# A four-layer trunk on one core: the first layer's sums of x two jobs later, two u tiles moved up, and the means of the two long pooling spans six places later

## The chip, the core and the metric

The kernel runs on one core of a Trainium2 chip. The core's engines each work through a queue of their own: TensorE (PE; its weight loads are shown as PEld), VectorE (DVE), ScalarE (ACT), GpSimd (POOL) and SyncE (SP), which here only issues DMAs. An instruction that waits for a semaphore holds up everything behind it in its engine's queue. The metric is the device time of one execution in microseconds (us).

## The reference

The reference is a trunk of four residual layers over 512 tokens of width 1024: pooling, gated convolution, latent attention, pooling; a last RMSNorm closes it. What matters here is the pooling layer (layers 1 and 4):

```python
xn = rms_norm(x, pool_norm[j])
u, z = jnp.split(xn @ w_in, 2, axis=-1)          # 1024 -> 2048 + 2048
for g, w in enumerate((2, 4, 8, 16)):            # four groups of 512 channels
    mean = trailing_mean(u[:, :, g], w)
    pooled.append(mean - u[:, :, g])
mixed = einsum('bsgc,gcd->bsgd', pooled, w_grp) * scale
x = x + (mixed * silu(z)) @ w_out
```

All inputs and the output are fp32.

## The kernel before

Activations lie with channels on the 128 partitions and the 512 tokens along the free dimension. Each fp32 operand of a matmul is split into a high part `h` (ACT copies it to fp32r) and a low part `l` (DVE subtracts), and each product is made of three matmuls (`mm3`, L260). So every weight chunk goes through ACT's `high` (L248) and DVE's `low` (L251) before PE can use it.

**Jobs and positions.** A `Stream` is a list of jobs. One job is a chunk of weights with its matmuls, and it has eight positions (0 to 7), one ahead of each k step. `step` (L215) loads the weights of the jobs one and two ahead, puts the preparation of the next job's weights into the positions of this job (high at 1, low at 2), and runs the matmuls. Everything that is to be done beside the matmuls is put down in a dictionary from position to functions; position 8 + p is position p of the next job, and so on. Work that is put down at the end of a job counts from the start of the next one. At one position the preparation of weights comes first. Within `Stream.run` the order in which PE, DVE and ACT get their instructions is the order in which this code issues them (`manual_schedule`, L231); the orders of POOL and SP are made by the scheduler.

**Chunk jobs** (`tile`, 24 matmuls with 512 columns) make one tile of u: 128 channels by 512 tokens. **Pair jobs** (`pair`, `seven`, L432) make two tiles of z at once out of seven products instead of eight, 84 matmuls with 256 columns. For those, x is needed in summed forms, `XNorm.forms` (L354): for each of four pairs of x tiles ACT makes g (L362), DVE four sums d1 and d2 (L366 to L369), ACT their high parts fh (L375) and DVE their low parts fl (L385). The weights need sums too, `prepare_pair` (L389): one block is loaded twice (s13, L117), a second one is added to it by an accumulating DMA that POOL issues (L121), and DVE and ACT make ah/al, sh/sl, ch/cl (positions 4 to 7) and, out of two further sums, th/tl (positions 10 and 11). The seven products use them in the order A11 (ah, al), S1 (sh, sl), A22, A12 (ch, cl), S2 and S4 (th, tl), S3.

**A pooling layer** (`pool_layer`, L590) runs jobs in the order of `ORDER`: uGI is tile I of group G of u, zGI a pair of z tiles, mGI half of the group's mixing matmul, h0 and h1 the two halves of the output projection (eight jobs each). In the first layer u00 and u01 are made together as the first job (`first_two`), and z00 and z01 are two chunk jobs each, since the summed forms aren't there yet. z10 is the first job that needs them.

**After a u tile** (`post_u`, L606): DVE multiplies it by the norm (`mul`, L583), POOL makes the trailing sums with one to four adds (`add`, L620; one for group 0, four for group 3), DVE makes the mean and subtracts the token (`mean`, L626 to L628), ACT makes the high part plh (L631) and DVE the low part pll (L634). The mixing matmul of the group reads plh and pll.

All these intermediate tiles, x with its split parts and the summed forms among them, come out of one set of 70 buffers (`up`, L69). Raw weight chunks have four buffers (`wr`).

The first two layers' jobs are in stream s1. The last layer's are in s2, whose jobs up to m21 are issued outside `manual_schedule` (L1262), so that there the scheduler makes DVE's, ACT's and PE's order too; from z30 on the order is the written one.

Of the kernel before, what the change touches and what calls it, by code (L numbers as in the profile page):

```python
# [64 lines left out]
def trunk_kernel(ctx: ExitStack, tc: tile.TileContext, a):  # L65
# [9 lines left out]
    def nm(s):  # L75
        cnt[0] += 1
        return f"{s}_{cnt[0]}"

    def ut(s, dt=F32, w=S):
        return up.tile([P, S + PAD], dt, tag="u", name=nm(s))[:, :w]  # L80
# [10 lines left out]
    def ps(s):  # L91
        return pp.tile([P, S], F32, tag="ps", name=nm(s))

    def f(t):
        return t.bitcast(F32)
# [55 lines left out]
    def pcol(name, i, p=None):  # L151
        return (par if p is None else p)[:, PC[name][0] + i : PC[name][0] + i + 1]
# [107 lines left out]
    def mm3(out, ah, al, bh, bl, first, last):  # L260
        nc.tensor.matmul(out, ah, bh, start=first, stop=False)  # L261
        nc.tensor.matmul(out, ah, bl, start=False, stop=False)  # L262
        nc.tensor.matmul(out, al, bh, start=False, stop=last)  # L263
# [318 lines left out]
    def tmul(dst, src, R):  # L582
        nc.vector.tensor_tensor(out=dst, in0=src, in1=R, op=ALU.mult)  # L583


    LATE = "u20 u21 m10 u22 u23 m11 h0 z20 z21 u30 u31 m20 u32 u33 m21 z30 z31 m30 m31 h1"
    ORDER = ("u00 u01 u02 u03 u10 u11 u12 u13 z00 z01 m00 m01 z10 z11 " + LATE,
             "u00 u01 u02 u03 z00 z01 u10 u11 m00 u12 u13 m01 z10 z11 " + LATE)

    def pool_layer(stream, j, xn, half, mid=None, at=(1, 3), pre=None):  # L590
# [12 lines left out]
        for g, w in enumerate(WINDOWS):  # L603
            pooled, szs = [], []

            def post_u(t, sign, g=g, w=w, pooled=pooled):  # L606
                u = up.tile([P, S + PAD], F32, tag="u", name=nm("u"))
                h, l = ut("plh", F32R), ut("pll", F32R)
                pooled.append((h, l))
                sums = []  # L610

                def mul():
                    nc.gpsimd.memset(u[:, :PAD], 0.0)
                    tmul(u[:, PAD:], t, ly.R[sign])
                    sums.append(u)

                def add(d):
                    cur, nx = sums[0], up.tile([P, S + PAD], F32, tag="u", name=nm("s"))
                    lo = 2 * d - 1
                    nc.gpsimd.tensor_tensor(out=nx[:, lo:], in0=cur[:, lo:], in1=cur[:, lo - d : S + PAD - d], op=ALU.add)  # L620
                    sums[0] = nx

                def mean():
                    cur, pd = sums[0], sums[0][:, PAD:]
                    hd = sp.tile([P, PAD], F32, tag="hd", name=nm("hd"))
                    nc.vector.tensor_tensor(out=hd, in0=cur[:, PAD : 2 * PAD], in1=con[:, C_INV + PAD * g : C_INV + PAD * (g + 1)], op=ALU.mult)  # L626
                    nc.vector.scalar_tensor_tensor(out=pd, in0=cur[:, PAD:], scalar=1.0 / w, in1=u[:, PAD:], op0=ALU.mult, op1=ALU.subtract)
                    nc.vector.tensor_tensor(out=pd[:, :PAD], in0=hd, in1=u[:, PAD : 2 * PAD], op=ALU.subtract)  # L628

                def high():  # L630
                    nc.scalar.activation(h, sums[0][:, PAD:], AF.Copy)  # L631

                def low():
                    nc.vector.tensor_tensor(out=l, in0=sums[0][:, PAD:], in1=f(h), op=ALU.subtract)  # L634

                adds = [lambda q=q: add(2**q) for q in range(g + 1)]
                return {0: [mul, *adds], 12: [mean], 14: [high], 16: [low]}

            def post_z(t, sign, szs=szs, plain=g == 0 and pre is not None):
                sz = ut("sz") if plain else t  # L640

                def scale():
                    tmul(sz, t, ly.R[sign])

                def gate():
                    nc.scalar.activation(sz, sz, AF.Silu)
                    szs.append(sz)

                return {0: [scale], 3: [gate]}

            def mix(mm, g=g, pooled=pooled, szs=szs):
                def run(wl, now):
                    for e in range(2):
                        i = 2 * mm + e
                        pm = ps("pm")
                        for k in range(4):
                            now(4 * e + k)
                            c = slice(k * 2 * P + e * P, k * 2 * P + (e + 1) * P)
                            mm3(pm, wl[0][:, c], wl[1][:, c], *pooled[k], first=k == 0, last=k == 3)
                        y, h, l = szs[i], ut("yh", F32R), ut("yl", F32R)  # L660
                        ys[g // 2].append((h, l))

                        def gated(pm=pm, y=y, i=i):
                            nc.vector.scalar_tensor_tensor(out=y, in0=pm, scalar=pcol(f"pool_scale{j}", 4 * g + i), in1=y, op0=ALU.mult, op1=ALU.mult)

                        def high(h=h, y=y):
                            nc.scalar.activation(h, y, AF.Copy)  # L667

                        def low(h=h, l=l, y=y):
                            nc.vector.tensor_tensor(out=l, in0=y, in1=f(h), op=ALU.subtract)  # L670

                        (stream.later if e else now).put({0: [gated], 3: [high], 4: [low]} if e else {5: [gated], 6: [high], 7: [low]})

                stream.add(CHUNK, wg[g, mm], run)

            for i in range(4):
                u_[g, i] = lambda g=g, i=i, post_u=post_u: ly.tile(stream, wu[4 * g + i], post_u)
            for i in range(2):
                z_[g, i] = lambda g=g, i=i, post_z=post_z: (ly.pair if g or pre is None else two_tiles)(stream, wz[2 * g + i], (post_z, post_z), mid and mid(g, i))
                m_[g, i] = lambda mix=mix, i=i: mix(i)  # L680
            if g == 0 and pre is not None:
                u_[0, 0] = lambda post_u=post_u: stream.add(None, None, lambda w, now: ly.done(stream, *[(post_u, t, 1) for t in pre()]))
                u_[0, 1] = lambda: None
        for c in ORDER[j].split():
            if c[0] == "h":
# [420 lines left out]
    s1, s2 = Stream(), Stream()  # L1106
# [7 lines left out]
    xn0 = XNorm("pool_norm0")  # L1114
# [3 lines left out]
    def split_w(m, hf, c, copy):  # L1118
        src, (h, l) = raw0[m, hf][:, c], w0[m, hf]
        copy(h[:, c], src)  # L1120
        nc.vector.tensor_tensor(out=l[:, c], in0=src, in1=f(h)[:, c], op=ALU.subtract)

    def first_two():

        pre = [ps("pt") for _ in range(2)]
        for k in range(KD):
            hf = k // 4
            c = slice((k % 4) * P, (k % 4 + 1) * P)
            for m in range(2):
                if k % 4 == 0:  # L1130
                    w0[m, hf] = ut("wh", F32R), ut("wl", F32R)
            if k == 0:
                split_w(0, 0, slice(0, P), nc.vector.tensor_copy)
                xn0.plain(k)
                split_w(1, 0, slice(0, P), nc.vector.tensor_copy)
                for m in range(2):
                    split_w(m, 0, slice(P, S), nc.vector.tensor_copy if m == 0 else nc.scalar.copy)
            else:
                xn0.plain(k)
                if k == 4:  # L1140
                    for m in range(2):
                        split_w(m, 1, slice(0, S), nc.scalar.copy)
            for m in range(2):
                wh, wl = w0[m, hf]
                if k == m == 0:
                    xh, xl = xn0.xs[0]
                    nc.tensor.matmul(pre[0], wh[:, c], xh, start=True, stop=False)
                    nc.tensor.matmul(pre[0], wl[:, c], xh, start=False, stop=False)
                    nc.tensor.matmul(pre[0], wh[:, c], xl, start=False, stop=False)
                    continue  # L1150
                mm3(pre[m], wh[:, c], wl[:, c], *xn0.xs[k], first=(k == 0), last=(k == KD - 1))
            if k >= 2:
                xn0.st.add(xt[k - 2])

        for m in range(KD - 2, KD):
            s1.later.put({0: [lambda m=m: xn0.st.add(xt[m])]})
        s1.later.put({3: [xn0.st.close]})
        for kk in range(KK):
            s1.later.put(xn0.forms(kk), 48 + 8 * kk)
        return pre  # L1160

    pool_layer(s1, 0, xn0, half, at=(3, 5), pre=first_two)
# [221 lines left out]
```

## Time and profile before

| what | value |
|---|---|
| time, median of 3 runs | 1491.59 us |
| the three runs | 1488.02, 1491.59, 1491.71 us |
| the profiled execution | 1488.14 us |
| its span, first to last instruction | 1486.4 us |
| mean granted clock of TensorE | 0.992 |

The profile was taken from one execution, which was near the faster of the runs. Its span leaves out 1.7 us around it. A row of the timeline reads: start, duration, engine, line, operation, output<-inputs, shapes, count, and in brackets how long the engine was idle before and what ended that. A row of the table of stretches reads: the stretch, its length, the busy time of PE (and number of instructions), PEld, DVE, ACT and POOL, then TensorE's granted clock, the DMA share and GB/s. A row of the view of waits reads: engine, what it was to do, for whom it waited: total, times, longest.

PE starts the first layer's jobs at these times (us from the start of the span): z00's two tiles at 54.93 and 60.46, z01's at 72.16 and 80.28, m00 at 87.08, z10 at 98.21, z11 at 108.13, u20 at 118.08, h0 at 151.41, m21 at 247.30, z30 at 252.82, m30 at 278.49.

### The profile page before, as it was taken

To read this page: it belongs to the slowest core of one execution; us is meant where nothing else is said; L and a number is where in the kernel's file an instruction comes from. 1 tells how busy PE (TensorE), PEld (TensorE's weight loads), DVE (VectorE), ACT (ScalarE), POOL (GpSimd) and SP (SyncE) were. 2 spreads that over 40 slices of the span, in tenths; PEclk is the share of its full clock that TensorE was granted. 3 is DMA by queue.
4 is the path that set the end of the run, shared out by engine and by line. 5 is a ranking of instruction groups with operands and counts; after the bars stand their busy time and mean duration, and the time that the engine had idled before them with its cause. 6 is when DMAs were issued, how large, how long until landed. Compare 5 with 4: busy or idle time off the path is not lost. (4 is left out here: it accounts for less than half of the span.)

```text
span 1486.4 us, 22441 instructions
## 1 busy us (share of the span) xinstructions
PE 1442.5 (97%) x8560; PEld 1271.0 (86%) x8560; DVE 1090.3 (73%) x1771; ACT 685.1 (46%) x1174; POOL 254.7 (17%) x291
## 2 busy tenths in 40 slices
PE   9899998999999999999999999999999999999898
PEld 6688797987999889999879987888888898888786
DVE  6885556749999879999688977677755588655773
ACT  4353242435555426555355655555633355323352
POOL 3402206021001000010211001111201132310502
PEclk9999999999999999999999999999999999999999
DMA  6143344425777357776236742122122443343431
GB/s 231 57 121 121 101 127 99 142 75 123 178 185 192 129 135 184 187 183 177 93 97 170 169 137 82 44 69 85 44 85 85 114 128 97 131 114 107 119 114 57
DMA packets 65147, 181.71 MB, mean 122 GB/s; under 512 B 8080, under 2 KB 8080, under 8 KB 65040
## 3 DMA queue, kind: packets, MB, share of 16 engines
q1 hardware_dynamic: 56688, 151.44, 33.4%
q0 software_dynamic: 7488, 27.27, 10.7%
q10 hardware_dynamic: 864, 1.57, 0.3%
q8 instruction: 67, 1.10, 0.3%
q14 instruction: 40, 0.33, 0.1%
HBM read 173.70 MB, written 2.10 MB: 118 GB/s over the span
## 5 line engine op out<-in xcount | busy, mean ns | idle before, releaser
L251 DVE TENSOR_TENSOR wl<-wr,wh 128x1024 fp32r<-128x1024 f32 (+1 forms) x140 | 173.3, 1238 | 52.5 <-ACT wh L248 52.0
L248 ACT ACTIVATE wh<-wr 128x1024 fp32r<-128x1024 f32 (+1 forms) x140 | 144.4, 1034 | 139.6 <-PE o L262 47.7
L263 PE MATMUL o<-yh,wl 128*128 128x512 f32 x384 | 151.1, 394 | 1.9 <-DVE wl L251 1.9
L262 PE MATMUL o<-yl,wh 128*128 128x512 f32 x384 | 151.2, 394 | 0.2 <-DVE yl L670 0.2
L261 PE MATMUL pt<-xh,wh 128*128 128x512 f32 x367 | 145.9, 398 | 5.6 <-ACT wh L248 5.2
L261 PE MATMUL o<-yh,wh 128*128 128x512 f32 x384 | 151.2, 394 | 0.1
L263 PE MATMUL pt<-xh,wl 128*128 128x512 f32 x367 | 145.1, 396 | 4.0 <-DVE wl L251 3.9
L262 PE MATMUL pt<-xl,wh 128*128 128x512 f32 x367 | 145.4, 396 | 1.0 <-DVE xl L352 0.9
L443 ACT ACTIVATE kept<-bv 128x256 f32<-128x256 f32 x52 | 19.9, 382 | 169.5 <-PE bv L429 137.4
L263 PEld LDWEIGHTS o<-yh,wl 128*128 128x128 f32 x384 | 72.1, 188 | 19.4 <-DVE wl L251 2.8
L261 PEld LDWEIGHTS pt<-xh,wh 128*128 128x128 f32 x367 | 69.4, 189 | 22.3 <-ACT wh L248 6.1
L263 PEld LDWEIGHTS pt<-xh,wl 128*128 128x128 f32 x367 | 69.3, 189 | 22.4 <-DVE wl L251 6.9
L262 PEld LDWEIGHTS o<-yl,wh 128*128 128x128 f32 x384 | 72.2, 188 | 17.1 <-DVE yl L670 0.5
L261 PEld LDWEIGHTS o<-yh,wh 128*128 128x128 f32 x384 | 72.0, 188 | 16.9 <-ACT yh L667 0.5
L262 PEld LDWEIGHTS pt<-xl,wh 128*128 128x128 f32 x367 | 69.5, 189 | 17.8 <-DVE xl L352 2.6
L399 DVE TENSOR_TENSOR sl<-s,sh 128x1024 fp32r<-128x1024 f32 x52 | 64.6, 1242 | 22.1 <-ACT sh L396 22.1
L121 POOL DMA_DIRECT2D s<-in_conv_in x30 | 26.0, 866 | 310.0 <-DMA s<-in_conv_in 95.4
L285 POOL TENSOR_TENSOR sq<-sq,sq 128x512 f32<-128x512 f32 x25 | 41.2, 1649 | 203.4 <-ACT sq L279 203.1
L399 DVE TENSOR_TENSOR al<-wr,ah 128x1024 fp32r<-128x1024 f32 x52 | 64.2, 1234 | 15.4 <-ACT ah L396 13.4
L620 POOL TENSOR_TENSOR s<-u 128x527 f32<-128x527 f32 x32 | 48.9, 1527 | 154.3 <-DVE u L583 146.1
L620 POOL TENSOR_TENSOR s<-s 128x525 f32<-128x525 f32 (+2 forms) x48 | 66.1, 1377 | 14.5 <-PE pm L262 11.2
L443 ACT ACTIVATE kept<-bx 128x512 f32<-128x512 f32 x104 | 50.9, 490 | 37.1 <-PE bx L429 37.1
(308 smaller groups left out, 4576.2 us busy)
## 6 DMA issues: line engine op xcount, KB each, us to landing
wr<-in_conv_in SPq DMA_DIRECT2D x34, 512.0 KB, 4.5
wr<-in_pool_out SPq DMA_DIRECT2D x32, 512.0 KB, 3.3
wr<-in_pool_u SPq DMA_DIRECT2D x30, 512.0 KB, 3.5
s<-in_conv_in SPq DMA_DIRECT2D x60, 256.0 KB, 3.9
s<-in_conv_in POOLq DMA_DIRECT2D x30, 512.0 KB, 7.0
wr<-in_pool_z SPq DMA_DIRECT2D x18, 512.0 KB, 4.5
wr<-in_pool_grp SPq DMA_DIRECT2D x16, 512.0 KB, 3.4
wr<-in_conv_out SPq DMA_DIRECT2D x16, 512.0 KB, 3.3
```

The source lines that it names most:

```text
L121: return (r, r4, s13), {4: [lambda: nc.gpsimd.dma_start(s13, src[:, :CH], accum_op=ALU.add)]}
L248: nc.scalar.activation(h, raw, AF.Copy)
L251: (nc.gpsimd if pool else nc.vector).tensor_tensor(out=l, in0=raw, in1=f(h), op=ALU.subtract)
L261: nc.tensor.matmul(out, ah, bh, start=first, stop=False)
L262: nc.tensor.matmul(out, ah, bl, start=False, stop=False)
L263: nc.tensor.matmul(out, al, bh, start=False, stop=last)
L285: eng.tensor_tensor(out=self.sum, in0=self.sum, in1=sq, op=ALU.add)
L399: return lambda: nc.vector.tensor_tensor(out=l, in0=t, in1=f(h), op=ALU.subtract)
L443: nc.scalar.activation(dst, src, AF.Copy)
L620: nc.gpsimd.tensor_tensor(out=nx[:, lo:], in0=cur[:, lo:], in1=cur[:, lo - d : S + PAD - d], op=ALU.add)
```

## The change

Three edits. In the order of the first layer, u20 and u21 come ahead of z10 and z11, right behind m01. The four calls of `forms` in the first layer are put down 16 positions later, which is two jobs: z10 has also moved two jobs back. And for groups 2 and 3, in both pooling layers, mean, high and low come six positions later. The arithmetic is the same.

```diff
     LATE = "u20 u21 m10 u22 u23 m11 h0 z20 z21 u30 u31 m20 u32 u33 m21 z30 z31 m30 m31 h1"
-    ORDER = ("u00 u01 u02 u03 u10 u11 u12 u13 z00 z01 m00 m01 z10 z11 " + LATE,
+    ORDER = ("u00 u01 u02 u03 u10 u11 u12 u13 z00 z01 m00 m01 u20 u21 z10 z11 m10 u22 u23 m11 h0 z20 z21 u30 u31 m20 u32 u33 m21 z30 z31 m30 m31 h1",
              "u00 u01 u02 u03 z00 z01 u10 u11 m00 u12 u13 m01 z10 z11 " + LATE)
...
                 adds = [lambda q=q: add(2**q) for q in range(g + 1)]
-                return {0: [mul, *adds], 12: [mean], 14: [high], 16: [low]}
+
+                late = 6 * (g // 2)
+                return {0: [mul, *adds], 12 + late: [mean], 14 + late: [high], 16 + late: [low]}
...
         for kk in range(KK):
-            s1.later.put(xn0.forms(kk), 48 + 8 * kk)
+            s1.later.put(xn0.forms(kk), 64 + 8 * kk)
         return pre
```

So the forms of the four pairs are made beside z01's two tiles, m00 and m01 (before: z00's two tiles and z01's two). A mean of group 2 or 3 now comes at position 2 of the second job behind the one in which its tile was multiplied (before: at position 4 of the first job behind it): u32's in z30 instead of m21, u33's in z31 instead of z30, u20's in z11.

## The prediction

> **What bounds the kernel now.** First the page: which engine is full.
>
> ```profile
> PE 1442.5 (97%) x8560; PEld 1271.0 (86%) x8560; DVE 1090.3 (73%) x1771; ACT 685.1 (46%) x1174; POOL 254.7 (17%) x291
> ```
>
> TensorE (PE) never rests for long, so any stall of it adds to the end and nothing else does. Second, the view of waits for PE: who made it stall, how often, and the longest.
>
> ```profile
> PE pt L261 <- ACT wh L248: 5.2, 2, 4.3
> PE bx L429 <- DVE al L399: 4.7, 2, 3.7
> PE bx L429 <- DVE tl L399: 4.4, 4, 1.9
> ```
>
> All of these are splits of weights that came late. Third, the table of stretches, cut at the starts of jobs on PE (z00's second tile begins at 60.46, z01's tiles at 72.16 and 80.28; 87.08 to 98.21 are m00 and m01, 108.13 is z11, 252.82 is z30 of the first layer, 1397.47 z30 of the last):
>
> ```profile
> 54.93:60.46 5.53, 5.53 (x26) 4.50 (x25) 5.39 (x12) 3.13 (x5) 2.46 (x5) 1.00 0.08 30
> 60.46:72.16 11.70, 5.97 (x26) 4.24 (x24) 11.03 (x18) 3.52 (x6) 5.09 (x5) 0.92 0.14 45
> 72.16:80.28 8.12, 8.08 (x24) 5.97 (x25) 7.95 (x17) 4.75 (x8) 1.05 (x1) 0.70 0.25 66
> 80.28:87.08 6.80, 5.81 (x25) 4.42 (x24) 6.60 (x12) 3.88 (x6) 0.00 (x0) 1.00 0.64 154
> 87.08:98.21 11.13, 11.13 (x49) 9.01 (x48) 9.22 (x15) 6.69 (x10) 0.88 (x2) 1.00 0.64 142
> 108.13:118.08 9.95, 9.95 (x86) 9.95 (x85) 7.37 (x11) 5.28 (x9) 0.00 (x0) 1.00 0.49 141
> 252.82:268.49 15.67, 12.00 (x86) 11.54 (x84) 15.29 (x20) 7.23 (x12) 6.82 (x6) 0.89 0.26 87
> 1397.47:1414.04 16.57, 12.41 (x86) 11.60 (x85) 13.13 (x17) 7.64 (x13) 8.08 (x8) 0.90 0.26 80
> ```
>
> The first number is the length, the third group from the right of the engines DVE's busy time. An undisturbed tile lasts 5.53, an undisturbed pair 9.95. So the three tiles from 60.46 lose 6.17 + 2.59 + 1.27 = 10.0 us, z30 of the first layer 5.7 and z30 of the last 6.6. VectorE (DVE) is busy throughout the first of these (11.03 of 11.70): there it is the bound.
>
> **Part 1: the sums two jobs later.** The timelines of PE, DVE, ScalarE (ACT) and GpSimd (POOL) around the largest stall:
>
> ```profile
> 62.51 0.50 PE L263 MATMUL pt<-xh,wl 128*128 128x512 f32 x1 [1.42 <-DVE wl L251]
> 72.16 0.80 PE L261 MATMUL pt<-xh,wh 128*128 128x512 f32 x1 [4.31 <-ACT wh L248]
> 62.38 1.28 DVE L366 SCALAR_TENSOR_TENSOR d<-x,par,g 128x256 f32<-128x256 f32 x1
> 66.50 0.69 DVE L634 TENSOR_TENSOR pll<-s,plh 128x512 fp32r<-128x512 f32 x1
> 67.10 0.17 DVE L626 TENSOR_TENSOR hd<-s,con 128x16 f32<-128x16 f32 x1
> 68.13 1.28 DVE L385 TENSOR_TENSOR fl<-d,fh 128x512 fp32r<-128x512 f32 x2
> 69.33 0.17 DVE L626 TENSOR_TENSOR hd<-s,con 128x16 f32<-128x16 f32 x1
> 72.14 1.23 DVE L251 TENSOR_TENSOR wl<-wr,wh 128x1024 fp32r<-128x1024 f32 x1 [0.50 <-ACT wh L248]
> 70.53 0.63 ACT L631 ACTIVATE plh<-s 128x512 fp32r<-128x512 f32 x1 [1.59 <-DVE s L628]
> 71.06 1.04 ACT L248 ACTIVATE wh<-wr 128x1024 fp32r<-128x1024 f32 x1
> 64.66 1.12 POOL L620 TENSOR_TENSOR s<-s 128x525 f32<-128x525 f32 x1
> L366 DVE SCALAR_TENSOR_TENSOR d<-x,par,g x16: 476/479/1512, 62.4 to 1167.8; 128x256 f32<-128x256 f32 x16
> ```
>
> Read it backwards: PE waits for ACT's wh (71.06), which stands in ACT's queue behind plh (70.53), which waits for the mean on DVE (69.33 to about 70.3). Ahead of that mean DVE did the first pair's four sums (62.38 to 66.50, 4.1 us) and two low parts (68.13 to 69.33, 1.2 us). Both leave this place. Not all of it is won: a sum's usual time is 0.48, three of these took 1.28, because POOL's adds ran at that time, and whatever stands there next meets the same adds. I charge three waits of about 0.8. From 62.4: plain low part 0.6 (66.50 to 67.10), two means of 1.0 (67.10 to 68.13), 2.5 of such waiting: 67.5; plh and wh (0.63 and 1.04) end at 69.1. PE is idle from 67.85 (72.16 less 4.31): 1.3 us remain, and wl, 1.2 us after wh where the third matmul wants it 0.46 after, adds 0.8. The stall of 1.42 at 62.51 lies ahead of the sums and stays with its restart, 1.7.
>
> Does the clock fall too? Two windows of the clock and one more, in the table of stretches:
>
> ```profile
> 59.97:63.39 3.42, 2.00 (x9) 1.31 (x8) 3.42 (x4) 0.25 (x1) 3.33 (x3) 1.00 0.00 0
> 66.80:70.21 3.41, 1.05 (x5) 0.53 (x3) 3.31 (x8) 1.08 (x2) 0.00 (x0) 1.00 0.00 0
> 70.21:77.04 6.83, 4.84 (x11) 3.35 (x12) 6.16 (x15) 4.01 (x7) 0.00 (x0) 0.50 0.26 69
> ```
>
> After 3.41 us with PE busy for 1.05 the clock was 0.50 for 6.83; after 2.00 of 3.42 it stayed. The changed window would have about 3.4 - 2.1 = 1.3 busy, nearer the first: I charge one half-speed window, 1.7 us. The Trainium skill, "TensorE: Matmul & The Clock Gate", section "What's actually happening", says that half clock comes after at least one idle window of about 3.4 us; taken literally no window would be lost here and the sum would be 1.7 lower, 1475.6. The trace speaks against the literal reading: 1.05 of 3.41 was no idle window, and half clock followed.
>
> So of 10.0 us, 1.7 + 1.3 + 0.8 + 0.3 for restarts + 1.7 = 5.8 remain: **won 4.2** (bounds 2 to 8.3). The second tile of z01 keeps no stall: its split has 2.9 us of sums and low parts fewer ahead of it.
>
> Where do the sums go? The third and fourth fall on m00 and m01, where DVE has 9.22 of 11.13 busy. In come 2 x 2.9, and a split of u20's weights, 1.2; out goes z10's preparation, about 4.5 (1.2, 1.2 and three of 0.7). That is 11.7 in 11.13: full, 0.6 late, absorbed by u20 and u21. I charge 0.3 (0 to 3). No DMA moves with the sums; u20's and u21's loads go to SP's queue ahead of z10's, whose buffers are free by the low parts of z01 and m00.
>
> **Part 2: u20 and u21 before z10 and z11.** PE's work is the same. Their adds, three for each tile, of 1.1 us (64.66) to 1.9 us, ran on POOL beside a DVE with little to do; now they run beside z10's and z11's preparation, and each add can hold up one DVE instruction by up to its 1.1 us. z10's first tl is wanted 5.92 us into the pair (four of its seven products, 9.95 / 7 = 1.42 each, and the third matmul), z11's likewise, and z11 gets u20's mean (1.0) ahead of its tl:
>
> ```profile
> 112.33 0.68 DVE L399 TENSOR_TENSOR tl<-wr,th 128x512 fp32r<-128x512 f32 x1
> ```
>
> It ended at 112.95, 4.8 into z11; with 1.0 of mean and up to 1 of lateness from z10, 6.8: 0.9 late. For z10 0.2. **Cost 1.1** (0 to 6.6, if all six adds delay the path by 1.1). The Trainium skill, "GPSIMD Engine Reference", section "8. Key points", says that GpSimd shares SBUF interfaces with VectorE and contends with instructions that have two SBUF inputs; all splits of a pair are such. By that rule every one of the six adds would be paid for, which is rival (a).
>
> **Part 3: means six places later.** The first layer's z30, where DVE stood still for POOL:
>
> ```profile
> 240.85 1.21 DVE L251 TENSOR_TENSOR wl<-wr,wh 128x1024 fp32r<-128x1024 f32 x1
> 242.09 0.80 SPq L117 DMA_DIRECT2D s<-in_pool_z  x2
> 247.38 0.87 POOL L121 DMA_DIRECT2D s<-in_pool_z  x1 [8.21 <-DMA s<-in_pool_z]
> 252.94 0.11 POOL L613 MEMSET u<- 128x16 f32 x1
> 253.03 0.18 DVE L626 TENSOR_TENSOR hd<-s,con 128x16 f32<-128x16 f32 x1 [4.85 <-POOL u L613]
> 255.61 1.21 DVE L399 TENSOR_TENSOR al<-wr,ah 128x1024 fp32r<-128x1024 f32 x1
> 264.22 0.68 DVE L399 TENSOR_TENSOR tl<-wq,th 128x512 fp32r<-128x512 f32 x1
> ```
>
> POOL waits 8.21 us to issue the accumulating load of a pair, since that pair's plain loads (242.09) had to wait for a buffer that DVE's wl (240.85) freed. u32's adds queue behind it and end at 252.94; the mean, and behind it al, wait for them. With the change the mean stands in z30 itself, behind al, sl, cl and the sums. DVE goes on at 248.2 (253.03 less 4.85). From al to the first tl it needed 264.2 - 255.6 = 8.6; a plain low part (0.6) leaves, the mean (1.0) comes: 9.0, with 0.7 for m21's first half and 0.8 for a POOL add 258.7, against 252.82 + 5.92 = 258.7 wanted. On the edge; I charge 0.6 (0 to 2). **Won 5.7 - 0.6 = 5.1.** Should the adds end later than about 257, the wait is back, now inside the pair. For z31, with u33's mean ahead of its tl, I charge 0.3.
>
> The same in front of h0 and of u33:
>
> ```profile
> PE o L263 <- DVE wl L251: 1.9, 2, 1.2
> PE pt L263 <- DVE wl L251: 0.4, 1, 0.4
> 149.99 0.69 DVE L583 TENSOR_TENSOR u<-pt,R 128x512 f32<-128x512 f32 x1 [7.51 <-PE pm L262]
> ```
>
> The shorter of the two in the first row (0.7) follows u23's multiplication, which waits for a buffer of m11: it stays. The 1.2 has u22's mean before it, which now comes behind that wl. u33's 0.4 goes as well. **Won 1.6.**
>
> In the last layer DVE's order up to z30 isn't written out, it is made by the scheduler:
>
> ```profile
> 1394.55 1.91 POOL L620 TENSOR_TENSOR s<-u 128x527 f32<-128x527 f32 x1 [4.78 <-DVE u L583]
> 1400.14 0.17 DVE L626 TENSOR_TENSOR hd<-s,con 128x16 f32<-128x16 f32 x1 [3.34 <-POOL u L613]
> ```
>
> The wait is the same, and here u32's adds also began late because DVE came late to u32's multiplication. With the mean in z30, whose order is written out, I take what z30 of the first layer keeps, 0.6, and as much again and half for ACT's order, 1.5: **won 6.6 - 1.5 = 5.1** (0 to 6.6).
>
> **Sum:** 4.2 + 5.1 + 1.6 + 5.1 - 0.3 - 1.1 - 0.3 = 14.3 us. The profiled execution took 1488.14 (span 1486.4 and 1.7 around it), near the lowest of the runs shown (1488.02); their median, 1491.59, is 3.45 higher. From the profile 1473.8, from the median 1477.3. I forecast the median: **1477**, in its own range 1469 to 1484.
>
> **Rivals.** (a) *The backlog only moves*: sums in m00 and m01 and adds beside z10 and z11 put those splits late. For it: DVE's 9.22 of 11.13. Against: u20 and u21 are light jobs. Price: six adds of 1.1 and two half-speed windows of 1.7, 10.0, of which 1.1 is counted: 1486. (b) *The last layer's gain is hidden*: the scheduler puts the moved means where DVE waits as before. For: its order there is its own. Then 5.1 fewer: 1482. (c) *The sums aren't what held wh up*: the change in the first layer misses, 4.2 fewer, 1481. For: POOL's adds stay. Against: 5.3 us of sums lie on the chain above. (d) *The mean's wait comes back inside the pairs*, with nothing behind it but tl: five places (z11, z30 and z31 of the first layer, z30 and z31 of the last). Price each 4.85 and a half window, 6.5. It decides from three of them on: 19.6, **1497, slower**. For: u32's adds end at 252.94 and 1400.1. Against: DVE gets to those means some 4 us into the pair.
>
> **How the numbers follow.** Forecast 0.65, (b) 0.14, (a) 0.10, (c) 0.06, (d) 0.05. About 0.3%, 4.5 us, is what a measurement here can tell: faster means under 1487.1. The forecast gives 0.64 of its 0.65 to that, (b) 0.13, (c) 0.05, (a) 0.04: faster 0.86; same 0.08, half of it from (a); slower 0.06. The range goes from 1467 (no half window, z30 without remainder) to 1486 and leaves out (d), half of (a) and a little below.
>
> **What would show it.** Right: the stretch of z01's first tile short of 8 us with a stall of 1 to 2.5 ahead; no DVE wait of over 2 us for POOL before al; both z30 at 10 to 12 us. Wrong: DVE waiting for POOL ahead of tl; z10 or z11 well over 10 us; the last layer's z30 still over 14.

## The result and the profile after

| | before | after |
|---|---|---|
| time, median | 1489.88 us (4 runs, 1488.02 to 1491.71) | 1477.87 us (4 runs, 1475.29 to 1478.50) |
| the profiled execution | 1488.14 us, span 1486.4 | 1477.38 us, span 1475.6 |
| mean granted clock | 0.992 | 0.995 |

The ratio is 0.9916, 95% interval [0.9904, 0.9929]: 12.0 us faster, 0.8%. The forecast was 1477 us. The time is met, but partly by luck: the sum of 14.3 us was 2.3 too large, and the median from which it was taken, 1491.59 of three runs, was 1.7 higher than that of four.

The page of the kernel after, its line of busy times:

```profile
PE 1437.4 (97%) x8560; PEld 1268.4 (86%) x8560; DVE 1094.1 (74%) x1771; ACT 684.6 (46%) x1174; POOL 260.4 (18%) x291
```

TensorE is still the bound: 38 us of its span is not matmul, where before it was 44. POOL is busy 5.7 us longer with the same 291 instructions, but 2.3 of this is one add, u20's first (4.25 us beside z10's preparation, 1.90 before), so the total doesn't say where the missing part of the forecast went.

The view of waits for PE, after (for whom, total, times, longest):

```profile
PE bx L423 <- ACT kept L443: 4.4, 3, 2.9
...
PE pt L261 <- ACT wh L248: 2.3, 2, 1.5
PE bx L429 <- DVE al L399: 1.1, 1, 1.1
```

The wait for wh fell from 5.2 to 2.3, its longest from 4.3 to 1.5; the one for al from 4.7 to 1.1. The one that grew most is the wait for `kept`, 1.5 before and 4.4 now. `kept` (L443) is ACT's copy of a product out of a PSUM bank that PE wants again; it is a light instruction that stands in ACT's queue, so one asks what held ACT up.

The stretches of the kernel after, cut, as in the prediction, where PE's jobs begin, so that a stall ahead of a job counts with the stretch before it (z00's second tile at 61.03, z01's at 69.87 and 76.32, m00 to u21 from 82.14, z10 and z11 from 104.37, h0 from 146.53, z30 and z31, and the last layer's z30 and z31); columns as before:

```profile
61.03:69.87 8.84, 5.97 (x25) 4.24 (x23) 8.20 (x12) 2.26 (x4) 5.83 (x5) 1.00 0.18 59
69.87:76.32 6.45, 5.92 (x25) 4.54 (x25) 6.16 (x12) 3.59 (x6) 0.00 (x0) 1.00 0.26 83
76.32:82.14 5.82, 5.81 (x25) 4.43 (x24) 5.69 (x11) 3.36 (x6) 0.00 (x0) 1.00 0.29 90
82.14:104.37 22.23, 22.23 (x97) 17.98 (x96) 21.99 (x35) 13.02 (x19) 5.97 (x4) 1.00 0.60 142
104.37:124.38 20.01, 20.01 (x169) 19.89 (x168) 15.78 (x21) 10.52 (x18) 6.67 (x7) 1.00 0.42 135
146.53:192.00 45.47, 44.77 (x193) 36.00 (x192) 24.72 (x32) 12.16 (x14) 6.41 (x8) 1.00 0.44 117
245.04:259.24 14.20, 11.73 (x85) 11.31 (x84) 12.48 (x15) 6.71 (x11) 5.10 (x4) 0.88 0.28 93
259.24:269.72 10.48, 10.20 (x87) 10.00 (x86) 9.23 (x16) 5.81 (x10) 0.00 (x0) 1.00 0.40 123
1387.01:1402.84 15.83, 11.77 (x85) 11.36 (x84) 13.44 (x16) 7.04 (x12) 7.99 (x7) 0.89 0.29 99
1402.84:1413.41 10.57, 10.14 (x87) 9.94 (x86) 9.34 (x16) 5.80 (x10) 0.00 (x0) 1.00 0.42 121
```

And two stretches of the kernel before that the prediction had no need of (z10 and z11; h0):

```profile
98.21:118.08 19.87, 19.87 (x169) 19.86 (x168) 15.80 (x22) 11.08 (x19) 0.11 (x1) 1.00 0.44 137
151.41:199.03 47.62, 45.44 (x194) 35.81 (x192) 25.72 (x32) 12.26 (x14) 6.61 (x8) 1.00 0.44 112
```

Set side by side, and beside them what the prediction charged:

| stretch | before | after | won | forecast |
|---|---|---|---|---|
| z00's second tile to m00 | 26.62 | 21.11 | 5.5 | 4.2 |
| m00, m01, u20, u21 (four tiles' time, 22.2) | – | 22.23 | 0.0 | –0.3 |
| z10 and z11 | 19.87 | 20.01 | –0.1 | –1.1 |
| h0 | 47.62 | 45.47 | 2.2 | 1.2 |
| z20 to m21 | 53.79 | 53.04 | 0.8 | 0.4 |
| z30, first layer | 15.67 | 14.20 | 1.5 | 5.1 |
| z31, first layer | 10.00 | 10.48 | –0.5 | –0.3 |
| z30, last layer | 16.57 | 15.83 | 0.7 | 5.1 |
| z31, last layer | 9.95 | 10.57 | –0.6 | in 5.1 |
| sum | | | 9.4 | 14.3 |

The spans differ by 10.8; the 1.4 that the table lacks lies mostly in the middle layers, which the change doesn't touch and where the profile of before happens to hold one more window of half clock (from 923.54 and from 937.20, against one from 915.47). So everything came in at or above its forecast but the last pairs of each layer: the two z31 lost 0.5 and 0.6, and the two z30 kept 4.2 and 5.9 us of their loss where I had charged 0.6 and 1.5.

Why did z30 keep it? The timeline of the kernel after around the first layer's z30 (start, duration, engine, line, operation):

```profile
242.56 1.73 DVE L399 TENSOR_TENSOR al<-wr,ah 128x1024 fp32r<-128x1024 f32 x1
244.87 1.42 DVE L399 TENSOR_TENSOR sl<-s,sh 128x1024 fp32r<-128x1024 f32 x1
246.22 1.55 DVE L399 TENSOR_TENSOR cl<-wq,ch 128x512 fp32r<-128x512 f32 x1
247.69 1.54 DVE L402 TENSOR_TENSOR wr<-s,wr 128x512 f32<-128x512 f32 x1
249.26 1.67 DVE L403 TENSOR_TENSOR wq<-wr,wq 128x512 f32<-128x512 f32 x1
252.12 0.16 DVE L626 TENSOR_TENSOR hd<-s,con 128x16 f32<-128x16 f32 x1
253.13 0.69 DVE L399 TENSOR_TENSOR tl<-wr,th 128x512 fp32r<-128x512 f32 x1
...
250.96 0.63 ACT L396 ACTIVATE th<-wq 128x512 fp32r<-128x512 f32 x1 [1.07 <-DVE wq L403]
251.50 0.58 ACT L443 ACTIVATE kept<-bx 128x512 f32<-128x512 f32 x1
...
243.34 1.88 POOL L620 TENSOR_TENSOR s<-u 128x527 f32<-128x527 f32 x1
245.29 5.09 POOL L620 TENSOR_TENSOR s<-s 128x525 f32<-128x525 f32 x3
...
252.13 0.39 PE L423 MATMUL bx<-fh,th 128*128 128x256 f32 x1 [1.23 <-ACT kept L443]
253.87 0.58 PE L429 MATMUL bx<-fh,tl 128*128 128x256 f32 x1 [1.23 <-DVE tl L399]
```

DVE no longer waits for POOL here; it is busy 12.48 of 14.20 us. But cl and the two sums (L402, L403) took 1.5 to 1.7 us each where a 128x512 split usually takes 0.68, and they did so exactly while POOL made u33's four adds (243.34 to 250.38). Those adds are not new beside DVE's work. The same stage of the kernel before:

```profile
253.25 1.49 DVE L627 SCALAR_TENSOR_TENSOR s<-s,u 128x512 f32<-128x512 f32 x1
254.77 0.92 DVE L628 TENSOR_TENSOR s<-hd,u 128x16 f32<-128x16 f32 x1
257.41 1.41 DVE L399 TENSOR_TENSOR sl<-s,sh 128x1024 fp32r<-128x1024 f32 x1
258.74 1.76 DVE L399 TENSOR_TENSOR cl<-wq,ch 128x512 fp32r<-128x512 f32 x1
...
253.13 1.06 POOL L620 TENSOR_TENSOR s<-u 128x527 f32<-128x527 f32 x1
254.27 5.69 POOL L620 TENSOR_TENSOR s<-s 128x525 f32<-128x525 f32 x3
```

There too u33's adds (253.13 to 259.96) cost DVE 2.8 us over the usual lengths, but 1.5 of it in the mean (L627 and L628, usually 0.69 and 0.17), and the two sums of the weights ran free at 0.68 and 0.69. After the change the mean has left this place, and the adds take their 2.9 us from sl, cl and both sums, all of them on the way to tl.

The sums now end late, so ACT's th waits for the last sum (1.07), `kept` stands behind th, and PE waits 1.23 for it. Then the mean (252.12) stands ahead of tl on DVE, and PE waits 1.23 again. And two windows of the clock, in the same kernel's stretches:

```profile
249.87:253.29 3.42, 1.53 (x11) 1.12 (x9) 3.35 (x7) 2.20 (x5) 0.51 (x1) 1.00 0.46 153
253.29:256.70 3.41, 2.83 (x13) 2.83 (x14) 2.86 (x4) 1.33 (x4) 0.00 (x0) 0.50 0.51 169
```

With PE busy 1.53 of 3.42 us in one window, the next ran at half clock: 1.7 us more. The two waits of 1.23 and this add up to the 4.2.

### The profile page after: what moved, and what is told of

Same layout as the page of the kernel before. It is cut to its first block, busy times and chain, and to the rows that moved or that the text cites. A ratio compares the mean times of both kernels' runs of the same rounds, so it can differ in the third digit from the quotient of the medians.

```text
span 1475.6 us, 22436 instructions
## 1 busy us (share of the span) xinstructions
PE 1437.4 (97%) x8560; PEld 1268.4 (86%) x8560; DVE 1094.1 (74%) x1771; ACT 684.6 (46%) x1174; POOL 260.4 (18%) x291
## 5 line engine op out<-in xcount | busy, mean ns | idle before, releaser
L443 ACT ACTIVATE kept<-bv 128x256 f32<-128x256 f32 x52 | 19.9, 382 | 167.2 <-PE bv L429 133.7
L620 POOL TENSOR_TENSOR s<-s 128x525 f32<-128x525 f32 (+2 forms) x48 | 69.5, 1448 | 9.6 <-PE pm L262 6.1
L443 ACT ACTIVATE kept<-bx 128x512 f32<-128x512 f32 x104 | 50.9, 490 | 38.6 <-PE bx L429 38.6
```

The lines of the kernel that those rows point to most:

```text
L443: nc.scalar.activation(dst, src, AF.Copy)
```

## The experiments

**Theory A**: what z30 keeps comes from u33's adds on POOL, which stretch DVE's splits of z30's weights. **Theory B**: it comes from the mean that now stands in z30 ahead of tl, with nothing to do with the adds. And for the first layer's start: is it the sums, the tiles moved up, or both?

**1. The means alone.** The kernel before with only `late`:

```diff
-                return {0: [mul, *adds], 12: [mean], 14: [high], 16: [low]}
+                late = 6 * (g // 2)
+                return {0: [mul, *adds], 12 + late: [mean], 14 + late: [high], 16 + late: [low]}
```

> Only the means, high and low parts of groups 2 and 3 come six positions later; order and sums of x as before. If the parts of the change add up as the two traces' stretches have them (first layer's z30 -1.5, z31 +0.5, h0 -2.1, z20 to m21 -0.8, last layer's z30 and z31 -0.1), the time is 4.0 us below before, about 1486, and the stretch of the three tiles from z00's second on stays 10 us over. Rival, that the means are worth what the prediction charged (11 us in all): about 1479.

Measured: 1481.69 us, ratio 0.9952 [0.9934, 0.9970], 7.1 faster. The stretch of z30 in this kernel's first layer:

```profile
249.15:261.16 12.01, 10.45 (x85) 10.03 (x84) 11.35 (x15) 5.97 (x10) 4.27 (x3) 1.00 0.32 111
```

That is 3.1 us more than expected: z30 is 2.2 shorter than with the whole change, as no half-speed window fell into it (clock 1.00, where the whole change had 0.88), and h0, at 44.50, is 1.0 shorter.

**2. Tiles and sums without the means.** The changed kernel with `late` at 0:

```diff
-                late = 6 * (g // 2)
+                late = 0
```

> Only the sums of x two jobs later with u20 and u21 ahead of z10 and z11; the means as before. If the parts add up: 5.4 us below before, about 1484.5; z01's first tile waits 1 to 2 us with no half clock; z10 and z11 together stay within 0.3 of 19.9; z30 of the first layer stays at 15 to 16 with its wait for POOL. Rival, that the adds of u20 and u21 cost z10 or z11 once their means come earlier: over 20.5 for the two.

Measured: 1483.94 us, ratio 0.9968 [0.9957, 0.9979], 4.8 faster. z30 keeps its old wait for al (3.72). 0.9952 times 0.9968 is 0.9920, against 0.9916 of the whole change: the two parts add up. The stretches z00's second tile to m00, and z10 with z11, of this kernel:

```profile
60.62:83.00 22.38, 18.98 (x74) 14.45 (x72) 21.29 (x36) 9.86 (x15) 5.83 (x5) 0.92 0.21 76
105.21:125.23 20.02, 20.02 (x170) 19.92 (x169) 17.85 (x25) 11.03 (x19) 4.91 (x5) 1.00 0.42 135
```

Here the half-speed window after the stall did come (0.92), and the stretch won 4.2, to the tenth what the prediction charged with one such window. z10 and z11 take the same 20.02 without u20's mean ahead of z11's tl: that mean costs nothing.

**3. Without u33's adds.** The four trailing sums of u33 are left out in both pooling layers, so that u33's mean is made of u itself; everything else is the changed kernel:

```diff
-                adds = [lambda q=q: add(2**q) for q in range(g + 1)]
+                adds = [lambda q=q: add(2**q) for q in range(g + 1)] if len(pooled) < 4 or g < 3 else []
```

> The changed kernel without POOL's four adds for u33, in both pooling layers (u33's mean is then made of u itself). Theory A, that in z30 DVE's splits and POOL's adds of u33 hold each other up and this keeps z30 slow: z30 of the first layer falls from 14.2 to 10 to 11 us, DVE's split of s, ch and the two sums there take 1.2, 0.7, 0.7 and 0.7 again, and z30 of the last layer falls from 15.8 to 12 or less; the time is 5 to 8 us under the changed kernel's. Theory B, that u32's mean ahead of tl does it: z30 of the first layer stays above 13.

Measured: 1468.24 us (one run), span 1466.5. Its timeline in z30, beside the rows of the kernel after:

```profile
243.82 1.21 DVE L399 TENSOR_TENSOR sl<-s,sh 128x1024 fp32r<-128x1024 f32 x1
244.96 0.68 DVE L399 TENSOR_TENSOR cl<-wq,ch 128x512 fp32r<-128x512 f32 x1
245.56 0.68 DVE L402 TENSOR_TENSOR wr<-s,wr 128x512 f32<-128x512 f32 x1
246.27 0.69 DVE L403 TENSOR_TENSOR wq<-wr,wq 128x512 f32<-128x512 f32 x1
```

and its stretches of z30, first layer and last:

```profile
244.71:254.63 9.92, 9.92 (x86) 9.92 (x85) 8.74 (x15) 5.86 (x10) 0.00 (x0) 1.00 0.39 134
1382.47:1393.40 10.93, 10.30 (x85) 10.02 (x84) 10.07 (x16) 6.49 (x11) 2.25 (x3) 1.00 0.40 144
```

Theory A holds in the first layer. The four instructions shrink from 1.42, 1.55, 1.54 and 1.67 to 1.21, 0.68, 0.68 and 0.69, 2.9 us in all, z30 goes from 14.20 to 9.92 and from 15.83 to 10.93. The mean still stands ahead of tl there and alone costs PE nothing (no wait in the first layer's z30): theory B needs the adds. The instruction that reads PSUM (L666, 0.74 in the kernel after) is not stretched.

**4. The means eight places later**, which puts the mean behind z30's tl, adds and all:

```diff
-                late = 6 * (g // 2)
+                late = 8 * (g // 2)
```

> The changed kernel with the means of groups 2 and 3 eight instead of six positions later, so that in z30 and z31 they stand behind tl. Theory B: in z30 of the first layer the stall of 1.2 for tl goes and with it the half-speed window (1.7), z30 at 11 to 11.5; z31 at 10.0. Theory A: the wait for kept, 1.2 us, which hangs on the sums of the weights beside u33's adds, stays, and z30 remains at 12 or more, though the mean's 1.0 us leave. Time: 3 to 5 us under the changed kernel by B, 1 to 3 by A.

Measured: 1473.00 us, ratio 0.9897 [0.9882, 0.9913]. The stretches of z30 in its first layer and in its last:

```profile
244.02:255.40 11.38, 10.46 (x86) 10.04 (x85) 11.28 (x14) 6.19 (x11) 4.64 (x3) 1.00 0.32 115
1384.35:1398.35 14.00, 12.01 (x85) 11.60 (x84) 13.38 (x16) 7.12 (x12) 7.37 (x7) 0.88 0.32 112
```

The wait for tl falls from 1.23 to 0.21 and takes the first layer's half-speed window with it; the wait for `kept` (0.71) stays, and so does one in the last layer (1.96). What is left in z30 is theory A's part, 11.38 - 9.92 = 1.5 us; what went, 2.8, came of both together. z31 takes 10.02. Run again on another chip: 1472.56 us, 0.9886 [0.9873, 0.9900]; there the last layer's z30 has the same wait (1.95) without a half-speed window and takes 12.49 instead of 14.00.

> The kernel late8 once more, beside the two that follow. About 1473, 15 us under before.

**5. The changed kernel again**, to stand beside the next three and to see whether the half-speed window after z01's stall comes every time.

> The changed kernel itself, on the chip of the three kernels beside it. About 1477.5, 11 to 12 us under before. Its stall of 1.5 and 0.5 us at z01's first tile brings a half-speed window in some executions and in others not (the run with the order alone had one there, the changed kernel's profile none), so the runs may spread by 1.7 us.

Measured: 1477.05 us, 0.9926 [0.9912, 0.9939]. This profile had that window, the first one didn't, with the same two stalls.

**6. u33 moved ahead of m20**, so that its adds run earlier, away from z30:

```diff
-    LATE = "... u30 u31 m20 u32 u33 m21 z30 ..."
+    LATE = "... u30 u31 u32 u33 m20 m21 z30 ..."
```

> The changed kernel with u33's job ahead of m20 in both pooling layers, so that POOL's four adds for u33 run beside m20, where DVE has little to do, and are over before z30 is prepared; u33's mean then falls on z30, u32's on m21. Theory A (DVE's splits and POOL's adds hold each other up): z30 of the first layer at 10 to 11, of the last at 10.5 to 12.5, 7 to 9 us under the changed kernel, about 1469.5. Theory B (the mean ahead of tl): 12 or more for both, since a mean still stands there.

A miss: 1479.92 us, 0.9946 [0.9934, 0.9959], slower than the change. Its z30 takes 13.60, from 246.33, and the last layer's 16.79. The timeline ahead of z30:

```profile
244.70 0.64 ACT L669 ACTIVATE yh<-O 128x512 fp32r<-128x512 f32 x1 [2.54 <-DVE O L666]
245.24 1.04 ACT L396 ACTIVATE ah<-wr 128x1024 fp32r<-128x1024 f32 x1
```

The adds ended at 246.8 and left the splits alone (al, at 247.31, took 1.21), but u32's mean and m20's gating now lay beside them, L666 came late, and z30's ah stood behind ACT's wait of 2.54 for it. The stretch of adds must lie somewhere, and here it hit what comes just ahead of the pair.

**7. The same, with only group 2's means late**:

```diff
-                late = 6 * (g // 2)
+                late = 6 * (g == 2)
```

> The same with the means of group 3 at their old place (12, 14, 16 behind the multiplication), group 2's six later: u33's mean then stands in m21 behind adds that are over, and nothing stands ahead of tl. A: z30 at 10 in the first layer and 10 to 11 in the last, z31 at 10.0, another 1 to 2 us under u33_early. If u33's adds are still under way in m21, DVE waits for POOL there as before, and it is slower than u33_early.

A miss as well: 1483.22 us, 0.9967 [0.9954, 0.9979]. DVE waits 1.49 for POOL with u32's mean, u33's adds begin only when u32's are done (241.47) and run beside m20's gating, ah comes only at 248.87, and PE waits 4.33 for it. The second guess of the expectation came true, that it would be slower than u33_early.

**8. The sums alone**, without the tiles:

```diff
-            s1.later.put(xn0.forms(kk), 48 + 8 * kk)
+            s1.later.put(xn0.forms(kk), 64 + 8 * kk)
```

> Before with the sums of x two jobs later and nothing else: z10 follows m01 at once, so DVE has in m00 and m01 the 9.2 us that it had, plus 2 x 2.9 of sums and low parts, 15 in 11.1. If the two moved u tiles are what makes the room: z10 starts its products 3 to 5 us late, with a half-speed window, and the 4 to 5.5 us won ahead of m00 are lost again: within 2 us of before. Rival, that the sums alone are enough: 4 to 5.5 us under before.

Between the two expectations: 1485.89 us, 0.9982 [0.9972, 0.9991], 2.3 to 2.7 faster. z01's stall is the small one (1.44 and 0.52), but z10 and z11, now two jobs nearer to the sums, take 21.17 instead of 19.87:

```profile
94.40:115.57 21.17, 20.83 (x169) 20.05 (x168) 18.04 (x26) 12.52 (x22) 0.11 (x1) 1.00 0.41 130
```

**9. The tiles alone**, with the sums at their old jobs:

```diff
-            s1.later.put(xn0.forms(kk), 64 + 8 * kk)
+            s1.later.put(xn0.forms(kk), 48 + 8 * kk)
```

(and `late` at 0).

> Before with u20 and u21 moved ahead of z10 and z11, the sums of x and the means at their old places. If the room in front of z01 comes from the sums alone, the stall of 4.3 us there stays and the time is within 1 us of before; the tiles alone are worth nothing. Rival: the tiles bring some of the 4.8 us of the run with order and sums by themselves.

Measured: 1489.99 us, 1.0005 [0.9996, 1.0014]: nothing, and the stall of 4.31 ahead of z01 stands. The tiles win nothing by themselves; together with the sums they make it 4.8 instead of about 2.5. They give DVE two light jobs in which to catch up before z10: the pairs account for 1.15 us of the difference (21.17 against 20.02); where the rest lies is open.

**10. u33's multiplication and adds one job later** (beside z30's second half, where z31's weights are prepared), in both layers, with the means six and eight places later:

```diff
+                if g == 3 and len(pooled) == 4:
+                    return {8: [mul, *adds], 20: [mean], 22: [high], 24: [low]}
```

> The changed kernel with u33's whole chain after its job put off by eight positions: multiplication and adds at the start of z30, mean, high and low at 20, 22, 24 (other means as changed). POOL's four adds then run behind z30's preparation instead of beside it. Theory A: z30 of the first layer at 10 to 10.8 as without the adds (9.9), al, sl, cl and the sums there at 1.2, 1.2, 0.7, 0.7, 0.7; z30 of the last layer at 11 to 12.5; z31 within 0.7 of 9.95, since the adds may now run beside its preparation, which has more time. 6 to 8 us under the changed kernel, about 1470. If the adds cost as much there: z31 at 12 or more, about 1476.

> u33_later with the other means of groups 2 and 3 at eight places later, so that u32's mean too stands behind tl. z30 at 10 in the first layer, 10.5 to 11.5 in the last, z31 at 10.0: 1 to 2 us under u33_later, about 1468.5, the fastest of all.

Measured: 1473.96 us, 0.9904 [0.9891, 0.9917], and 1473.27 us, 0.9892 [0.9879, 0.9906]. The first puts z30's cl and sums back to 0.68 each, as theory A says, but now a tl takes 1.54 and PE waits 0.99 for it; z30 takes 11.24 and z31 10.94. In the second z30 takes 9.95 and z31 12.1. The cost moves with the adds from one pair to the next, and neither beats the means eight places later, though about 1470 and 1468.5 had been expected: both are misses.

The fastest complete version is the changed kernel with eight places instead of six, level with the last one above: 1.0 and 1.1% under the kernel before in its two comparisons, and by the medians 4.5 to 4.9 us (0.3%) under the change, beside which it was never measured directly.

## Why the prediction was right or wrong

**What bounds the kernel: right.** TensorE stayed the bound, and the stretches above account for 9.4 of the 10.8 us that left the span.

**Part 1, the sums: right, with the mechanism as told.** A stall of 1.45 for wh and of 0.53 for wl stayed, where 1.3 and 0.8 were charged. The three waits for POOL's adds, charged at 2.5, came as well: pll took 1.55, two small steps of a mean 1.03 and 0.92, together 2.5 over their usual 0.68, 0.17 and 0.17. Only the half-speed window was left to chance: in the profile of the change it didn't come (5.5 won), in that of order and sums it did (4.2 won). That the sums make the stall, and not POOL's adds, is shown by the sums alone: the four adds stay beside that stretch (60.43 to 66.97 there), only the sums leave, and the stall falls from 4.31 to 1.44; rival (c) falls. The two DVE-heavy jobs, charged 0.3, cost nothing: 22.23 us is four tiles of 5.56, with DVE busy 21.99.

**Part 2, the adds beside z10 and z11: direction right, size too large.** 1.1 charged, 0.1 measured; rival (a) falls.

**Part 3, h0 and m21: right, too small.** 1.6 charged, 2.9 measured. The view of waits accounts for the 1.2 that is gone ahead of h0 (the wait of `o` for wl is down from 1.9 to 0.7); the remainder is a shorter busy time of PE in h0, 45.44 to 44.77. Both come from the means: with them alone h0 takes 44.50, with order and sums alone 47.58. Why PE's busy time shrinks is open.

**Part 3, the two z30: this is the step that failed.** I wrote "9.0, with 0.7 for m21's first half and 0.8 for a POOL add 258.7" and charged 0.6, and for the last layer 1.5. The wait that it meant to remove is gone: al no longer waits for POOL, and the path from al to tl decides, as forecast. That path was mis-sized. Set against the start of z30 (252.82 before, 245.04 after), the forecast's 258.7 is 250.9 in the kernel after; the first tl ended at 253.8, 2.9 us late, in two halves. From al's start to the end of tl it took 11.25 (242.56 to 253.81) where 9.0 and 0.8 were charged: not one instruction of the weights meets an add but sl, cl and both sums, besides al, which met the last of u32's (1.73 instead of 1.21). The 8.6 us taken from the kernel before held only 1.3 us of such waiting, since there the mean met the first adds. And al began 1.4 us later than the 248.2 and 0.7 of the forecast: u32's adds, which had run while DVE stood idle (247.99 to 253.00 before), now ran beside u31's mean, which took 3.3 us (237.11 to 240.38) instead of 1.0.

That made "on the edge" a miss of the edge: PE waited twice for 1.23, behind the sums and behind the mean, and paid a half-speed window besides, so that 4.2 us stayed; the upper bound that I gave, 2, was too low as well. The cause is shown for u33's adds: without them the path took 8.34 (241.51 to 249.85) and z30 9.92, without a stall. For the late start no run was made.

In the last layer something like it happened, with an order that the scheduler made. Its timeline in z30, kernel after:

```profile
1389.96 0.54 DVE L626 TENSOR_TENSOR hd<-s,con 128x16 f32<-128x16 f32 x1
1394.16 1.78 DVE L403 TENSOR_TENSOR wq<-wr,wq 128x512 f32<-128x512 f32 x1
...
1390.54 4.85 POOL L620 TENSOR_TENSOR s<-s 128x525 f32<-128x525 f32 x3
...
1397.15 0.58 PE L423 MATMUL bx<-fh,th 128*128 128x256 f32 x1 [2.87 <-ACT kept L443]
```

The mean (from 1389.96, 2.2 us with its three instructions) stands ahead of cl and of a sum here, though I had counted on "the mean in z30, whose order is written out"; PE waits 1.20 for cl. Then the adds, from 1390.54 to 1395.39, stretch the sum to 1.78, and PE waits 2.87 for `kept`. Rival (b), the last layer's gain hidden, therefore came true in its price (0.1 of 5.1 won, z31 included). Its mechanism was there in part: DVE still waits 4.65 for POOL ahead of al, now with u31's mean (3.76 before), while the wait of 3.34 that the prediction showed is gone. But that isn't what holds z30: without u33's adds DVE waits 4.57 there, and z30 takes 10.93. In that run the scheduler also put the mean behind cl and both sums (1387.55), so for the last layer it doesn't separate the adds from the mean; with the adds in place and the mean behind tl, z30 took 14.00 and 12.49.

**Rival (d)** had the right place, behind tl, but not the right cause: DVE doesn't wait for POOL in any of those pairs. Its mean ahead of tl is worth something only where the adds have made the pair late already; then it cost 2.8 us together with the clock, as the means eight places later show.

**The rule on GpSimd.** The Trainium skill, "GPSIMD Engine Reference", section "8. Key points", says that the two engines contend where DVE has two SBUF inputs. The trace agrees, with 1.55 beside adds and 0.68 without; in the first layer's z30 four instructions paid, though not every such instruction does (last section). In z10 and z11 a tl took 1.54 and an al 2.07, and PE lost nothing by it; DVE was busy for only 15.78 of 20.01 us there, which is likely the reason.

**The end of the sum.** 14.3 against 10.8 between the two spans and 12.0 between the medians. That the forecast of 1477 met 1477.87 is luck in good part: the four pairs of group 3 fell 8.8 us short (8.0 of it in the two z30), and what made up for it was 3.9 us more than forecast in the other stretches, 1.4 outside them, mostly one half-speed window fewer in the middle layers, and a starting median that was 1.7 too high. Of the signs named beforehand, z01's stall was right (6.45 us with a stall of 1.45 ahead); both z30 at 10 to 12 was not, and in the last layer DVE still waits over 2 us for POOL ahead of al. A sign of being wrong came: the last layer's z30 is over 14.

## What to carry to other kernels

When a wait goes, look at what the waiting engine will meet next, and with which instructions. Work that used to run while it stood still (u32's adds here) now runs beside it, and work that used to hit a harmless instruction (u33's adds, the mean) now hits the critical ones. Where two engines contend, allow for every instruction that overlaps, not for one, and ask how much of it the old duration already holds. A mean or other side work belongs behind the last instruction that the pair itself needs (here eight places instead of six, 1.0 to 1.1% instead of 0.7 to 0.8%). Moving the contending work earlier or later moves its cost, unless there is a stretch in which the other engine has slack.

## What was unexpected of the hardware

**The same stall costs a half-speed window or not, by chance of phase.** The stall of about 1.45 plus 0.53 us ahead of and in z01's first tile stood in eleven profiles; in six of them (tiles and sums without the means, the change run again, u33 ahead of m20, the sums alone, eight places later run again, and u33's adds later with eight places) the clock was halved after it, in five it was not. The windows, in the kernel with tiles and sums alone, where it was:

```profile
67.68:71.09 3.41, 1.43 (x6) 0.62 (x5) 2.91 (x5) 2.10 (x3) 0.00 (x0) 1.00 0.00 0
71.09:74.50 3.41, 3.41 (x10) 2.67 (x9) 3.12 (x9) 1.73 (x3) 0.00 (x0) 0.50 0.41 154
```

and in the kernel after, where it wasn't:

```profile
68.97:72.38 3.41, 1.98 (x8) 1.34 (x8) 2.87 (x5) 1.37 (x2) 0.00 (x0) 1.00 0.12 18
```

The windows' ends lie differently against the stall from run to run, so that one holds 1.43 us of work or 1.98: the first begins 0.33 us before the stall for wh, the second 0.55 us after its start. With 1.05, 1.43 and 1.53 the clock fell, with 1.98 and 2.00 it didn't. In between PE's busy time, as the profile models it, does not decide: with 1.73 in the window the clock fell (eight places later run again, from 68.19), and elsewhere it did not with 1.73 (eight places later, from 922.57) or 1.75 (experiment 7, from 1393.77). The Trainium skill, "TensorE: Matmul & The Clock Gate", section "What's actually happening", speaks of an idle window; here windows that were 45 to 51% busy were enough. So this stall of 2 us carried a further 1.7 us in six profiles of eleven, and a single profile isn't proof that it was avoided.

**How much the two engines hold each other up, and which of them pays.** Beside adds, DVE's 128x512 operations with two SBUF inputs go from 0.68 to 1.55, 1.54 and 1.67 us in the first layer's z30, some 0.9 more each, and POOL's first add of a tile from 1.06 to 1.88. They take turns there: POOL's last three adds end at 247.22, 248.68 and 250.38, and cl and the two sums each end 0.55 us after one of them. I had expected a delay for one instruction, not for each in a row. But not every instruction beside an add pays: in the last layer's z30 cl took 0.68 beside u33's adds. And the same place of the same kernel can go either way. u20's first add beside z10's preparation, in the first profile of the change and in that of experiment 5:

```profile
100.45 4.25 POOL L620 TENSOR_TENSOR s<-u 128x527 f32<-128x527 f32 x1 [1.75 <-DVE u L583]
...
101.56 1.91 POOL L620 TENSOR_TENSOR s<-u 128x527 f32<-128x527 f32 x1 [2.50 <-DVE u L583]
```

In the first, al, sl, cl and a sum ran beside the add at 1.21, 1.22, 0.68 and 0.68, and POOL paid; in the second sl, cl and the sum took 2.09, 1.54 and 1.54 beside this add and the two that follow it. z10 and z11 together took 20.01 and 20.02 us. What decides between the two no run shows.
